# A two-layer encoder step on one core: the norms' element work at three sub-layer transitions put on VectorE alone, and the first group's read-out moved into a later m-tile

## The chip, the core and the metric

The kernel runs on one NeuronCore of a Trainium2 chip. The metric is the device time of one execution in microseconds (us), lower is better. An engine is called as the profile calls it: PE (TensorE, the matmul array), PEld (its weight loads), DVE (VectorE), ACT (ScalarE), POOL (GpSimd), SP (SyncE, which issues most DMAs).

## What is computed

The reference is one inference step of a trunk of two layers over 256 frames of a new stream and 16 frames each of 8 running streams, 384 tokens in all with 1024 features. Each layer has a mixer (even: stick-breaking attention and a gated short convolution; odd: a spatial gate and latent attention) and a squared-ReLU MLP. Around every sub-layer stand two RMS norms:

```python
h = rms_norm(x, p["mix_pre_g"][layer])
out = mixer(h)                                        # even or odd
x = x + rms_norm(out, p["mix_post_g"][layer])
h = rms_norm(x, p["ffn_pre_g"][layer])
x = x + rms_norm(sq_relu_mlp(h, w_up, w_down), p["ffn_post_g"][layer])
```

So between two sub-layers the output `out` is normed and added to `x`, `x` is normed again, and the next product starts. With two layers there are three such places inside the kernel: mixer 0 to MLP 0, MLP 0 to mixer 1, mixer 1 to MLP 1. They are called transitions here.

## The kernel before, in words

Activations lie with features on partitions: `x` is eight k-tiles of 128 features x 384 tokens. Every float32 product is made of three matmuls over two halves of each operand: a high half `h` (a rounded copy) and a low half `l` (the difference): `h*h`, `l*h`, `h*l`. Weights arrive in chunks of 512 KB by a DMA on SP; ACT casts a chunk into its high half (`whi`, line 98) and DVE subtracts to get its low half (`wlo`, line 99). Each of `raw`, `whi` and `wlo` is a ring of four buffers.

`dense` (line 296) makes one m-tile of the output after another, 8 k-tiles x 3 = 24 matmuls each over 384 columns, and reads each out with a function `evac` that its caller gives. `group` (line 271) makes the first four m-tiles of a projection side by side, so that its products of k-tile k need only that k-tile of `x`: per k-tile 8 matmuls with the high half of `x` and 4 with the low half, 96 in all. At its end all four are read out. PSUM has three tiles of tag `mm`, three of `at` and two of `aux`; the four m-tiles of a group and the next two of `dense` take all six of the first two tags.

A transition runs as follows. The last m-tile of the projection before it is squared (`OutNorm.put`, line 182), a product with ones sums the squares over the features (line 159), and ACT makes `rpost`, the reciprocal root, by Ln and Exp (lines 144, 145); meanwhile twelve matmuls that nobody reads keep PE at work (`keep_warm`, line 119). Then `Norms.prep` (line 232) does, per k-tile k: `t`, o scaled by `rpost` (line 215); `x`, added to x (line 218); `h`, the high half of gain times x, on ACT (line 221); `l`, the low half, on DVE (line 225); `s`, the square of x on ACT and its sum into `acc` on POOL (lines 168 to 172). For k = 0 the halves are made by a short way of four DVE operations (lines 242 to 245). `ORDER` (line 199) writes out in which order these steps follow on every engine; `keep` holds them to it. The other instructions (weight casts and splits) are placed between them by the framework's scheduler, which orders instructions by priority and by simulated readiness, gives out buffers, and makes the waits.

Before, `t` of k = 0 and 1, `x` of k = 0, 1, 3 and 5 and all additions of squares run on POOL, the other `t`, `x` and all `l` on DVE. When `acc` is complete, `pre_rstd` (line 264) splits it into halves (`acch` on ACT, `accl` on DVE), sums them over the features with two matmuls on PE and makes `rb` by Ln and Exp. Every read-out of the next projection multiplies by `rb`; the first one to be read out calls `pre_rstd`. In the MLP the read-out is `up` (line 402): DVE makes `h_r` (line 404), ACT its square `hh`, POOL its square again, DVE the low half `hl`. In the odd layer it is `lat` (line 699), for six m-tiles only: three of queries' latent (`qc`), two of keys' (`kv`), one of rotated keys, with the squares' sums of `qc` and `kv` for two more norms (`rkb`, `rqb`), behind which come the query products (`w_uq`); the spatial gate's product (`w_sv`) is cut into four chunks that are placed among them. `group` is used six times: at the kernel's start (`w_q`), in the three transitions (`w_up_r` twice, `w_lat_r`) and in the two output projections, whose read-out `OutNorm.put` needs no PE.

Of the kernel before, what the change touches and what calls it, by code (L numbers as in the profile page):

```python
# [15 lines left out]
P = 128  # L16
# [20 lines left out]
def encoder_step_kernel(ctx: ExitStack, tc: tile.TileContext, a):  # L37
# [26 lines left out]

# [1 line left out]
    xall = res.tile([P, KT, TOK], F32, name="x")  # L66
# [28 lines left out]

# [1 line left out]
    def split_into(hi, lo, src, eng=vec):  # L97
# [21 lines left out]
    def keep_warm(after, n):  # L119
        """PE work whose result nobody reads: an idle array drops to half its clock."""  # L120
        scratch = psum("aux")
        warm = identr.rearrange("p (r c) -> p r c", r=1).broadcast_to([P, NT, P])
        with tc.issue_after(after):
            for _ in range(n):
                mm(scratch[:, :TOK].rearrange("p (r c) -> p r c", r=NT), identr, warm, start=True, stop=True)
# [15 lines left out]

# [1 line left out]
    def rsqrt(out, src, n):  # L143
# [50 lines left out]
    class Norms:  # L194
        """x += the post-norm of o, which carries its gain; then the next sub-layer's pre-norm of x, its rstd left for
        later. Two k-tiles at a time: prep() before the products that need them, post() after."""

        # how the k-tiles follow one another on every engine: o scaled, x updated, x split in two, x squared
        ORDER = ("t1 x1 t0 x0 h1 t2 t3 x2 x3 l1 h2 s0 s1 l2 h3 t4 t5 x4 l3 s2 h4 s3 l4 x5 s4 h5 t6 x6 t7 x7 l5 s5 h6 h7 l6 "
                 "l7 s6 s7")  # L200

# [25 lines left out]
        def square(self, k):  # L227
            if k == 0:
                self.acc = wk.tile([P, TOK], F32, name="acc")
            self.last_add = square_acc(self.acc, x[k], k == 0, keep)  # L230

        def prep(self, c):
            if not self.o:
                for k in (2 * c, 2 * c + 1):
                    if k == 0:
                        vec.tensor_scalar(out=xs(k)[0], in0=x[k], scalar1=gain(self.g_pre, k), scalar2=None, op0=ALU.mult)
                    else:
                        self.hi(k)
                    self.lo(k)
            elif c == 0:  # L240
                h, l = xs(0)
                tt(out=self.b0, in0=self.b0, in1=self.r, op=ALU.mult)
                keep(tt(out=h, in0=self.a0, in1=self.b0, op=ALU.add))  # L243
                keep(tt(out=self.a0, in0=h.bitcast(F32), in1=self.a0, op=ALU.subtract))
                keep(tt(out=l, in0=self.b0, in1=self.a0, op=ALU.subtract))
                for step in self.ORDER.split():
                    k = int(step[1])
                    if step[0] == "t":
                        keep(self.scale_o(k, pool if k < 2 else vec))
                    elif step[0] == "x":  # L250
                        keep(self.add_o(k, pool if k in (0, 1, 3, 5) else vec))
                    elif step[0] == "h":
                        keep(self.hi(k))
                    elif step[0] == "l":
                        keep(self.lo(k))
                    else:
                        self.square(k)

# [10 lines left out]

# [1 line left out]
    def group(src, order, evac, norm=None, between=None, tags=("mm", "mm", "mm", "at")):  # L271
        """Four m-tiles side by side, the weights in chunks of two k-tiles."""
        pss = [psum(t) for t in tags]
        for i, c in enumerate(order):
# [14 lines left out]
            if norm:  # L289
                norm.post(c)  # L290
        for m, p_ in enumerate(pss):
            evac(m, p_[:, :TOK], ins.ins)
        wide["n"] = 4
        return ins.ins

    def dense(src, mts, rhs, nk, evac, eng=vec, tag=None):
        for i, m in enumerate(mts):
            p_ = psum(tag) if tag else psum_dense()
            for c in range(0, nk, KT):
                w = chunk(src[i] if nk <= KT else src[i, c // KT], eng=eng)  # L300
                for kk in range(min(KT, nk)):
                    k = c + kk
                    ins = mm3(p_[:, :TOK], cut(w, slice(kk * P, (kk + 1) * P)), rhs(k), k == 0, k == nk - 1)
            evac(m, p_[:, :TOK], ins.ins)

    def token_major(src, evac):
        """Tokens on partitions; stops after each of the four chunks' products."""
        pss = [psum("mm") for _ in range(NT)]
# [25 lines left out]

# [1 line left out]
    NF = 4 * KT  # L336
    LAST = 3

    def turn(k):
        """A tile of x from features to tokens on partitions, in its place."""  # L340
        pt = psum("aux")
# [4 lines left out]
    def down_last(hp, hh, hl):  # L346
        """The last product, its norm and the sum with x, tokens on partitions: one tile of tokens ends after another."""
        gb = hp.tile([P, D], F32, name="gb")
# [84 lines left out]

# [1 line left out]
    def softplus(hp, z, n, out, order=None, **dims):  # L435
# [8 lines left out]
    def even_layer(norm):  # L444
        rbs = []
        with tc.tile_pool(name="even", bufs=1) as hp:
# [21 lines left out]
            group(a["w_q"], range(4), qk, norm, between)  # L468
            rb, r = rbs
            wide["on"] = True  # L470
            dense(a["w_k"], range(4, 8), xs, KT, qk)
            wide["on"] = False
            load("ident", ident)
# [19 lines left out]
            def add_sums(z, sp, n, stop):  # L493
                """z -= the sums of sp over the keys that a row's key comes before, as two exact halves."""
                h, l = (hp.tile([P, 512], F32R, name=i, bufs=2)[:, :n] for i in ("sph", "spl"))
# [13 lines left out]
            for h in range(H):  # L509
# [3 lines left out]
                                 in_=q[p][rows, TP:].rearrange("p (b i) -> p b i", b=NB))  # L513
            # the sample's new keys against its queries, heads of one parity side by side
            po = psum("aux")
# [15 lines left out]
            nc.scalar.copy(att[:, :, TP:], po.rearrange("p (g t) -> p g t", g=NPAIR))  # L531
            # their sums, as exponents' bias for the past keys: [(h i), b]
            # (a key's row is zero but for its own stream)
            sps = hp.tile([P, P], F32, name="sps", tag="pm", bufs=2)
# [70 lines left out]
            for i in range(NB):  # L605
# [6 lines left out]
                if i % 2:  # L612
                    prompt_values(i // 2, ws[-2:])
            # gated short convolution, per tile of 128 channels
            NE = TP + 2 + NB * (TS + 2)
# [58 lines left out]

# [1 line left out]
    def rope(hp, src, dst, rows):  # L676
# [8 lines left out]
    def odd_layer(norm):  # L685
        rbs = []
        with tc.tile_pool(name="odd", bufs=1) as hp:
# [30 lines left out]
            keep(vec.tensor_copy(maskr, mask))  # L718
            rb, r = rbs
            wide["on"] = True  # L720
            dense(a["w_lat"], range(4, 6), xs, KT, lat)
            wide["on"] = False
            rkb = rstd_bcast([acck], 256, "rkb")
# [15 lines left out]

            # the spatial gate's values, tokens on partitions  # L740
            ln = hp.tile([P, 1024], F32, name="ln")
# [18 lines left out]

            # the prompt's queries and keys by head, 64 and 32 (rotated) together: rows 0-95 for even heads, 32-127 for odd
            q8 = [o[h][:, :TP] for h in range(H)]
# [7 lines left out]
            for p in range(NPAIR):  # L770
                with tc.issue_after(norm.last_add):
                    pool.memset(q8[2 * p][96:128, :], 0.0)
                    pool.memset(q8[2 * p + 1][0:32, :], 0.0)
            # the sample's: two heads' 64 in a tile's last columns; the rotated 32 as [high, low, high], [r, b, h, i]
            qn = [o[2 * p][:, TP:] for p in range(NPAIR)]
# [30 lines left out]

            # prompt keys out of the latent
            def prompt_keys():
# [11 lines left out]

            # the new latent rows, tokens on partitions
            p_ = psum("aux")
# [5 lines left out]
            vt = [hp.tile([P, 512], F32, name=f"vt{t}") for t in range(2)]  # L828
            # prompt values out of the latent
            def prompt_latent_values():  # L830
# [10 lines left out]

            # absorbed queries of the sample tokens: [c, ct, b, h, i]
            ql = []
# [69 lines left out]

            # sample attention over the past and the new rows
            def rope_keys(b):
                """Two streams' rotated keys, as [high, high, low]."""
                raw, hi = raw_tile()[0:96, :], hi_tile()[0:96, :]
# [99 lines left out]

            # the spatial gate's steps lie between the samples
            ln_at, su_at = (1, 2, 4), (2, 3, 4, 5)
# [35 lines left out]

            # spatial gating
            new_xs()
# [24 lines left out]
def _arrays(i):  # L1082
# [55 lines left out]

    # constants of the shapes
    c["ident"] = np.eye(P, dtype=f)  # L1140
# [57 lines left out]
```

## Time and profile before

| | us |
|---|---|
| median of three runs | 959.29 |
| lowest and highest run | 959.02, 960.0 |
| span of the profiled execution | 959.2 |
| PE busy in it | 927.6 (97%) |
| DVE busy | 559.6 (58%) |
| ACT busy | 392.5 (41%) |
| POOL busy | 210.7 (22%) |

The profile is of one execution; its span, from the first to the last instruction, is 959.2 us and lies within the range of the timed runs, 0.1 us under their median. Times in rows are us from the start of that span. A row of the timeline gives start, duration, engine, line, operation, output and inputs, a count when rows are merged, and in brackets the engine's idle time before it with what ended it. The duration of a matmul includes its way through the array; matmuls overlap, and the time from one start to the next is what one costs.

### The profile page before, as it was taken

The page shows a single profiled execution, that of the slowest core. Times are in us where ns is not written, and L with a number is a line of the kernel's source. Part 1 is how long each engine was busy: PE and PEld are TensorE (multiplying, and loading weights), DVE is VectorE, ACT ScalarE, POOL GpSimd, SP SyncE. Part 2 cuts the span into 40 slices and gives each one's busy share as a digit, 9 for nine tenths or more (in the row PEclk, how much of TensorE's full clock was granted, in tenths as well). Part 3 has the DMA queues.
Part 4 walks back from the last instruction along what each step waited for, and adds up shares of the span by engine and source line. Part 5 has one row for each costly group of instructions (what it writes and reads, how often), then busy time and mean ns, then how long its engine had stood idle before and what let it go on. Part 6 is the DMA issues. An engine that isn't in the chain of part 4 may idle for free.

```text
span 959.2 us, 13748 instructions
## 1 busy us (share of the span) xinstructions
PE 927.6 (97%) x5328; PEld 849.5 (89%) x5328; DVE 559.6 (58%) x798; ACT 392.5 (41%) x661; POOL 210.7 (22%) x236
## 2 busy tenths in 40 slices
PE   8999999989999999999979989999799999999997
PEld 6976679978999999999969779989699999888885
DVE  7457675578666643323396788664976666332234
ACT  6256553345333332222245665553453334222222
POOL 4200113345312210001055314003642212000000
PEclk9999999999999999999999999999999999999999
DMA  7957733323333433333322646454243333334322
GB/s 244 356 178 254 254 131 127 121 85 110 132 119 124 132 133 116 126 132 125 118 96 85 190 145 220 154 177 132 68 141 121 132 131 111 122 121 132 130 68 66
DMA packets 44593, 135.64 MB, mean 141 GB/s; under 512 B 5264, under 2 KB 10768, under 8 KB 44528
## 3 DMA queue, kind: packets, MB, share of 16 engines
q1 hardware_dynamic: 42128, 131.53, 41.4%
q0 software_dynamic: 816, 2.45, 0.7%
q8 instruction: 42, 0.69, 0.3%
q10 hardware_dynamic: 1584, 0.79, 0.3%
q14 instruction: 23, 0.19, 0.1%
HBM read 130.20 MB, written 3.89 MB: 140 GB/s over the span
## 4 chain that ended last, share of the span: by engine, by line
PE 87%; DVE 9%; issue 1%; ACT 1%; DMA 1%; SPq 0%; POOL 0%; DVEq 0%
PE ps_mm L135 10%; PE ps_mm L136 10%; PE ps_mm L137 10%; PE ps_at L135 8%; PE ps_at L136 8%; PE ps_at L137 8%; PE ps_mm L359 2%; PE ps_at L359 2%; PE ps_at L358 2%; PE ps_mm L357 2%; PE ps_mm L358 2%; PE ps_at L357 2%; PE ps_aux L982 2%; DVE o L215 2%; DVE xl L225 2%; PE ps_mm L288 1%
## 5 line engine op out<-in xcount | busy, mean ns | idle before, releaser
L99 DVE TENSOR_TENSOR wlo<-raw,whi 128x1024 fp32r<-128x1024 f32 (+3 forms) x200 | 264.9, 1327 | 246.5 <-ACT whi L98 245.2
L98 ACT CAST whi<-raw 128x1024 fp32r<-128x1024 f32 (+3 forms) x200 | 204.9, 1026 | 399.9 <-issue 137.6
L135 PE MATMUL ps_mm<-xh,whi 128*128 128x384 f32 x396 | 134.5, 340 | 0.0
L137 PE MATMUL ps_mm<-xh,wlo 128*128 128x384 f32 x396 | 133.9, 338 | 0.0
L136 PE MATMUL ps_mm<-xl,whi 128*128 128x384 f32 x396 | 133.7, 338 | 0.0
L172 POOL TENSOR_TENSOR acc<-acc,sq 128x384 f32<-128x384 f32 x48 | 66.8, 1392 | 203.5 <-ACT sq L171 200.7
L409 POOL TENSOR_TENSOR h<-h_r 128x384 f32<-128x384 f32 x64 | 58.5, 916 | 185.1 <-DVE h_r L404 185.1
L135 PE MATMUL ps_at<-xh,whi 128*128 128x384 f32 x284 | 95.9, 338 | 0.0
L136 PE MATMUL ps_at<-xl,whi 128*128 128x384 f32 x284 | 95.7, 337 | 0.0
L137 PE MATMUL ps_at<-xh,wlo 128*128 128x384 f32 x284 | 95.6, 337 | 0.0
L135 PEld LDWEIGHTS ps_mm<-xh,whi 128*128 128x128 f32 x396 | 74.4, 188 | 3.0 <-issue 1.9
L136 PEld LDWEIGHTS ps_mm<-xl,whi 128*128 128x128 f32 x396 | 74.4, 188 | 2.1 <-issue 1.8
L137 PEld LDWEIGHTS ps_mm<-xh,wlo 128*128 128x128 f32 x396 | 74.3, 188 | 1.9 <-issue 1.7
L136 PEld LDWEIGHTS ps_at<-xl,whi 128*128 128x128 f32 x284 | 53.3, 188 | 0.0
L135 PEld LDWEIGHTS ps_at<-xh,whi 128*128 128x128 f32 x284 | 53.3, 188 | 0.0
L137 PEld LDWEIGHTS ps_at<-xh,wlo 128*128 128x128 f32 x284 | 53.3, 188 | 0.0
L285 PE MATMUL ps_mm<-xh,whi 128*128 128x384 f32 x132 | 45.7, 349 | 5.1 <-DVE xh L243 3.0
L286 PE MATMUL ps_mm<-xh,wlo 128*128 128x384 f32 x132 | 45.1, 344 | 1.8 <-DVE wlo L99 1.8
L288 PE MATMUL ps_mm<-xl,whi 128*128 128x384 f32 x132 | 32.5, 351 | 11.4 <-DVE xl L225 8.7
L135 PE MATMUL ps_mm<-hh,whi 128*128 128x384 f32 x128 | 43.2, 337 | 0.0
L136 PE MATMUL ps_mm<-hl,whi 128*128 128x384 f32 x128 | 43.2, 337 | 0.0
L137 PE MATMUL ps_mm<-hh,wlo 128*128 128x384 f32 x128 | 43.2, 337 | 0.0
(370 smaller groups left out, 1856.9 us busy)
## 6 DMA issues: line engine op xcount, KB each, us to landing
raw<-in_w_up SPq DMA_DIRECT2D x56, 512.0 KB, 3.5
raw<-in_w_down SPq DMA_DIRECT2D x32, 512.0 KB, 3.5
raw<-in_w_down_last SPq DMA_DIRECT2D x32, 512.0 KB, 3.5
kc<-in_sb_kT SPq DMA_DIRECT2D x16, 512.0 KB, 5.6
vc<-in_sb_v SPq DMA_DIRECT2D x16, 512.0 KB, 5.4
raw<-in_w_conv_in SPq DMA_DIRECT2D x12, 512.0 KB, 5.4
raw<-in_w_up_r SPq DMA_DIRECT2D x8, 512.0 KB, 3.5
raw<-in_ckvT SPq DMA_DIRECT2D x8, 512.0 KB, 4.3
```

The costliest lines, as they stand in the source:

```text
L98: nc.scalar.copy(hi, src)
L99: eng.tensor_tensor(out=lo, in0=src, in1=hi.bitcast(F32), op=ALU.subtract)
L135: mm(out, w[0], x_[0], start=start, stop=False)
L136: mm(out, w[0], x_[1], start=False, stop=False)
L137: return mm(out, w[1], x_[0], start=False, stop=stop)
L172: added = pool.tensor_tensor(out=acc, in0=acc, in1=sq, op=ALU.add)
L285: mm(p_[:, :TOK], w_[0], h, start=first, stop=False)
L286: mm(p_[:, :TOK], w_[1], h, start=False, stop=False)
L288: ins = mm(p_[:, :TOK], w_[0], l, start=False, stop=last)
L357: mm(out, hh[k][:, sl], hi, start=(k == 0), stop=False)
L358: mm(out, hh[k][:, sl], lo, start=False, stop=False)
L409: pool.tensor_tensor(out=h2, in0=h_r, in1=h_r, op=ALU.mult)
```

## The change

All three transitions: `t` and `x` run on DVE for every k. `ORDER` goes k by k from 1 to 7, with `l` one step behind `h`; squares (`s`, ACT alone) follow, and the additions of squares are steps of their own (`a`, DVE), put at the end together with k = 0's `t`, `x` and `s`. `acc` starts as the square of k = 1. `group` no longer reads out its m-tiles but leaves that in a list, `later`; the first m-tile of the `dense` that follows puts its own read-out there too; and in the second m-tile, after the matmuls of its k-tile 4 (`nk // 2`), the list is worked off, PE's instructions in it being ordered behind those matmuls. `rb, r = rbs` moves behind the `dense` call in both mixers. `norm.last_add`, behind which ten POOL memsets of the odd layer are ordered, is now a DVE instruction.

```diff
-        ORDER = ("t1 x1 t0 x0 h1 t2 t3 x2 x3 l1 h2 s0 s1 l2 h3 t4 t5 x4 l3 s2 h4 s3 l4 x5 s4 h5 t6 x6 t7 x7 l5 s5 h6 h7 l6 "
-                 "l7 s6 s7")
+        ORDER = ("t1 x1 h1 t2 x2 h2 l1 t3 x3 h3 l2 s1 t4 x4 h4 l3 s2 t5 x5 h5 l4 s3 t6 x6 h6 l5 s4 t7 x7 h7 l6 l7 a2 s5 a3 s6 "
+                 "a4 s7 t0 x0 a5 s0 a6 a7 a0")
...
         def square(self, k):
             if k == 0:
                 self.acc = wk.tile([P, TOK], F32, name="acc")
-            self.last_add = square_acc(self.acc, x[k], k == 0, keep)
+            square_acc(self.acc, x[k], k == 0, keep)
+
+        def square_alone(self, k):
+
+            if k == 1:
+                self.acc = self.sq[k] = wk.tile([P, TOK], F32, name="acc")
+            else:
+                self.sq[k] = wk.tile([P, TOK], F32, name="sq", tag="t15", bufs=4)
+            keep(act(out=self.sq[k], in_=x[k], func=AF.Square))
+
+        def add_square(self, k):
+            self.last_add = keep(tt(out=self.acc, in0=self.acc, in1=self.sq[k], op=ALU.add)).ins
...
                     if step[0] == "t":
-                        keep(self.scale_o(k, pool if k < 2 else vec))
+                        keep(self.scale_o(k, vec))
                     elif step[0] == "x":
-                        keep(self.add_o(k, pool if k in (0, 1, 3, 5) else vec))
+                        keep(self.add_o(k, vec))
...
+                    elif step[0] == "s":
+                        self.square_alone(k)
                     else:
-                        self.square(k)
+                        self.add_square(k)
...
+    later = []
+
     def group(src, order, evac, norm=None, between=None, tags=("mm", "mm", "mm", "at")):
...
-        for m, p_ in enumerate(pss):
-            evac(m, p_[:, :TOK], ins.ins)
+        def leave():
+            for m, p_ in enumerate(pss):
+                evac(m, p_[:, :TOK], ins.ins)
+
         wide["n"] = 4
-        return ins.ins
+        later.append(leave)
 
     def dense(src, mts, rhs, nk, evac, eng=vec, tag=None):
...
                     ins = mm3(p_[:, :TOK], cut(w, slice(kk * P, (kk + 1) * P)), rhs(k), k == 0, k == nk - 1)
-            evac(m, p_[:, :TOK], ins.ins)
+                    if i == 1 and k == nk // 2:
+                        with tc.issue_after(ins.ins):
+                            while later:
+                                later.pop(0)()
+            if i == 0 and later:
+                later.append(lambda m=m, p_=p_, ins=ins: evac(m, p_[:, :TOK], ins.ins))
+            else:
+                evac(m, p_[:, :TOK], ins.ins)
...
             group(a["w_q"], range(4), qk, norm, between)
-            rb, r = rbs
             wide["on"] = True
             dense(a["w_k"], range(4, 8), xs, KT, qk)
+            rb, r = rbs
...
             group(a["w_lat_r"], range(4), lat, norm)
             keep(vec.tensor_copy(maskr, mask))
-            rb, r = rbs
             wide["on"] = True
             dense(a["w_lat"], range(4, 6), xs, KT, lat)
+            rb, r = rbs
```

The rest of the diff removes comments and docstrings.

## Rows read from the trace of the kernel before

**Rows 1.** The page, its first part: busy time of each engine, share, instructions.

```profile
PE 927.6 (97%) x5328; PEld 849.5 (89%) x5328; DVE 559.6 (58%) x798; ACT 392.5 (41%) x661; POOL 210.7 (22%) x236
```

**Rows 2.** Windows, three transitions: length, PE, PEld, DVE, ACT, POOL busy, PEclk, DMA.

```profile
203.57:228.06 24.49, 19.12 (x102) 17.26 (x101) 21.79 (x25) 10.25 (x19) 17.14 (x13) 1.00 0.20 63
483.37:509.40 26.03, 20.69 (x103) 18.80 (x102) 22.94 (x26) 10.80 (x19) 19.44 (x17) 0.93 0.18 59
672.66:697.15 24.49, 19.14 (x102) 17.27 (x101) 21.78 (x25) 10.25 (x19) 17.15 (x13) 1.00 0.28 87
```

**Rows 3.** Timeline of ACT, steady state of MLP 0.

```profile
241.19 1.05 ACT L98 CAST whi<-raw 128x1024 fp32r<-128x1024 f32 x1 [0.27 <-PE ps_mm L136]
...
245.41 1.05 ACT L98 CAST whi<-raw 128x1024 fp32r<-128x1024 f32 x1 [1.62 <-PE ps_mm L136]
```

**Rows 4.** Timeline of PE, first transition: its five waits, then pre_rstd.

```profile
205.46 0.44 PE L285 MATMUL ps_mm<-xh,whi 128*128 128x384 f32 x1 [1.01 <-DVE xh L243]
208.03 0.79 PE L288 MATMUL ps_mm<-xl,whi 128*128 128x384 f32 x3 [0.90 <-DVE xl L245]
211.53 0.80 PE L288 MATMUL ps_mm<-xl,whi 128*128 128x384 f32 x3 [1.12 <-DVE xl L225]
219.57 0.45 PE L285 MATMUL ps_mm<-xh,whi 128*128 128x384 f32 x1 [0.54 <-ACT xh L221]
223.03 0.79 PE L288 MATMUL ps_mm<-xl,whi 128*128 128x384 f32 x3 [1.79 <-DVE xl L225]
228.06 0.34 PE L159 MATMUL ps_aux<-acch,ponesr 128*128 128x384 f32 x1
```

**Rows 5.** Timeline of DVE, first transition.

```profile
203.57 0.56 DVE L242 TENSOR_TENSOR b<-b,rpost 128x384 f32<-128x384 f32 x1
204.17 1.24 DVE L243 TENSOR_TENSOR xh<-a,b 128x384 fp32r<-128x384 f32 x1
...
214.51 0.55 DVE L218 TENSOR_TENSOR x<-x,o 128x384 f32<-128x384 f32 x1
214.98 0.60 DVE L225 SCALAR_TENSOR_TENSOR xl<-x,small,xh 128x384 fp32r<-128x384 f32 x1
215.51 1.21 DVE L99 TENSOR_TENSOR wlo<-raw,whi 128x1024 fp32r<-128x1024 f32 x1
```

**Rows 6.** Lines by form, 203 to 229: busy us, mean ns | idle before, releaser.

```profile
L172 POOL TENSOR_TENSOR acc<-acc,sq 128x384 f32<-128x384 f32 x7 | 9.6, 1368 | 5.2 <-ACT sq L171 5.0
...
L215 DVE TENSOR_TENSOR o<-o,rpost 128x384 f32<-128x384 f32 x6 | 7.2, 1229 | 0.0
...
L225 DVE SCALAR_TENSOR_TENSOR xl<-x,small,xh 128x384 fp32r<-128x384 f32 x7 | 5.5, 822 | 0.0
...
L221 ACT ACTIVATE xh<-x,small 128x384 fp32r<-128x384 f32 x7 | 4.3, 612 | 11.0 <-DVE x L218 5.9 <-POOL x L218 5.1
...
L218 DVE TENSOR_TENSOR x<-x,o 128x384 f32<-128x384 f32 x4 | 2.9, 724 | 0.1
...
L99 DVE TENSOR_TENSOR accl<-acc,acch 128x384 fp32r<-128x384 f32 x1 | 0.6, 561 | 2.5 <-ACT acch L98 2.5
...
L98 ACT CAST acch<-acc 128x384 fp32r<-128x384 f32 x1 | 0.5, 513 | 3.2 <-POOL acc L172 3.2
```

**Rows 7.** Windows, inside the second transition (columns as in rows 2).

```profile
503.00:506.40 3.40, 3.40 (x12) 3.40 (x13) 1.97 (x3) 0.73 (x2) 2.87 (x2) 0.50 0.10 23
```

**Rows 8.** Timeline of four engines, behind the second transition's group.

```profile
510.01 0.58 ACT L144 ACTIVATE rb<-ps_aux,epst 128x384 f32<-128x384 f32 x1
...
510.67 0.52 ACT L145 ACTIVATE rb<-rb 128x384 f32<-128x384 f32 x1
...
518.83 0.81 PE L159 MATMUL ps_aux<-acck,ones 128*128 128x384 f32 x2
...
524.83 0.52 PE L135 MATMUL ps_at<-qch,whi 128*128 128x384 f32 x2
...
510.14 0.56 DVE L99 TENSOR_TENSOR wlo<-raw,whi 128x384 fp32r<-128x384 f32 x1 [0.47 <-ACT whi L98]
...
510.31 0.31 POOL L772 MEMSET o<- 32x256 f32 x1
```

More of the change, by code (lines that the diff above doesn't have):

```diff
@@ L245, in prep @@
                 keep(tt(out=l, in0=self.b0, in1=self.a0, op=ALU.subtract))
+                self.sq = {}
                 for step in self.ORDER.split():
```

## The prediction
> **What bounds the kernel now.** The page's first part comes first: PE is busy 97% of the span [rows 1], so time can only come from places where PE stands still or runs slowly, or be lost there. The chain of waits and the table of waits then point to three such places, the transitions: from the sum that gives `rpost` to the last product of the next group of four m-tiles. The windows view [rows 2] shows their length: 24.49, 26.03 and 24.49 us, with VectorE busy 21.8 to 22.9 us and GpSimd 17 to 19 us of each. A group is 8 k-tiles x 12 products = 96 matmuls. At PE's steady pace, 4.22 us from one weight cast to the next, each after an m-tile of 24 products [rows 3], one product takes 0.176 us, so the group needs 16.9 us of the 24.49. PE's own timeline [rows 4] shows the rest: five waits of 1.01, 0.90, 1.12, 0.54 and 1.79 us, four on VectorE and one on an `xh` whose `x` came from GpSimd, plus filling up after each.
>
> Why VectorE is late is read from durations. The same 128x384 operation takes 0.55 to 0.60 us with GpSimd idle (L218 at 214.51, L225 at 214.98) and 1.24 us beside it (L243 at 204.17) [rows 5]; the group means, 1229, 822 and 724 ns, are mixtures of the two [rows 6]. So GpSimd's help is paid for twice: its own adds take 1.37 us [rows 6], and VectorE's operations beside them double.
>
> In the second transition the clock fell too: the granted clock is 0.50 from 503.0 to 506.4, the lower level, 1.2 GHz [rows 7], after a stretch with those five waits. That transition is 1.54 us longer than its twins [rows 2].
>
> **The change, part by part.** Set t = 0 where L242 starts (203.57 in the first transition, 483.37 in the second) [rows 5]. On VectorE an operation that needs the one before it starts 0.60 later (L242 to L243), an independent one 0.47 later (L218 to L225) and one behind an L225 0.53 later (L225 to L99) [rows 5].
>
> *GpSimd leaves.* Its 2 scalings, 4 residuals and 7 square sums move to VectorE: 13 operations at about 0.55. In return the 25 operations of the chain up to the last `xl` (4 of the head, 7 each of t, x, l) lose their neighbour. I take 0.55 to 0.60 for all of them; bounds are 0.55 (never a neighbour) and 1.24 to 1.36 (always), and the nearest rows are those with GpSimd idle, since nothing of the transition stays there.
>
> *PE's new course.* xh0 is ready at 0.60 + 0.56, and PE starts at 1.20 (before: 1.89) [rows 4]. xl0 comes at 2.4, in time for k=0's last four products. Then t1 at 2.27, x1 at 2.87 to 3.43, h1 on ScalarE 0.61 [rows 6] to 4.08: PE waits about 0.8 us and starts k=1 at 4.13. From here VectorE needs t + x + l = 0.60 + 0.47 + 0.53 = 1.60 us per k-tile against PE's 12 x 0.176 = 2.11: PE leads the pace. The group ends at 4.13 + 7 x 2.11 = 18.9 instead of 24.49: **5.6 us saved**. The cover: two to three weight splits of 1.2 us [rows 5] in VectorE's queue still leave the last `xl` at about 17, needed at 18.2. Were that slack gone, each missing microsecond would be PE's.
>
> *The square sums now end late.* After l7 VectorE still has 7 adds, t0 and x0: 9 x 0.6 = 5.4, and another split or two: 22.4 to 23.5; with the cast and the low half of `acc` (0.51 + 0.56) [rows 6] and handovers 23.6 to 24.7. Read out at the group's end as now, that would hold PE from 18.9 on. The deferral puts the two products of pre_rstd behind k=4 of the second m-tile: 18.9 + 4.2 + 2.6 = 25.7. Slack 1 to 2 us, so the sums cost nothing while it lasts.
>
> *The wait that comes in.* Four PSUM tiles of the group and two of m-tiles fill all six; the third m-tile needs the first read out. `rb` comes at 25.7 + 0.35 + Ln and Exp 1.2 [rows 8] = 27.3, the read-out lasts to 27.9; PE is through the second m-tile at 18.9 + 8.4 + 0.35 = 27.6. PE waits 0.25. Later read-outs need to keep one tile per 4.2 us, which the steady state does already. Behind these waiting read-outs on VectorE stand only the weight splits of later chunks. **Net per MLP transition 5.6 - 0.25 = 5.35, twice: 10.7 us**; bounds 3 (slack gone) and 5.6.
>
> *The second transition* (odd layer) gains 5.6 + 1.54 = 7.1 at the group's end, if with fewer waits the clock stays up. But behind it lies a chain of short steps that the deferral feeds later: only two m-tiles follow. pre_rstd starts at 483.37 + 25.7 = 509.1 and `rb` ends some 0.3 us before the 511.19 of now [rows 8]; then come five read-outs, their squares and GpSimd's adds, and the sum for `rkb` can start at about 515.6 (now 518.83, behind PE's own queue) [rows 8]; the query products start 6.0 us later (524.83 now) [rows 8]: 521.7. PE has the first chunk of `w_sv` as filling from 511.6 to 516 and then nothing for up to 5 us. So at most 3.2 us get through in this reading. Such an idle stretch may bring the lower clock for a while as in [rows 7], whose price was 1.54. I take 2.3, between 1.5 and 3.2; outer bounds 0 and 7.1.
>
> The Trainium skill, "TensorE: Matmul & The Clock Gate", section "What's actually happening", says that the throttled clock is the default and that activity releases it. The fall in this trace after a stretch of waits agrees; by that rule the lower clock moves from the transition to the queries, and the odd layer keeps about 1.5: the sum would be 947.1 instead of 946.3.
>
> *Edits at nothing.* Ten memsets of the odd layer were ordered behind GpSimd's last add; that add is VectorE's now, so nothing orders them and they may run during the transition. A 384-column split with two inputs took 0.56 beside one [rows 8], so they don't slow VectorE. The first group (`w_q`) and the two output projections also have their read-outs deferred. PE has two m-tiles of 8.4 us to run meanwhile; the projections' read-outs hold no PE work, so they are free to go at once, and their sum is asked for four m-tiles later. For `w_q`, the first key tile's output DMA on GpSimd's queue moves with the read-out, with the whole projection of `w_v` left before attention. I take 0, bounds -0.3 (better) and +1.0 (its `rb` shares ScalarE with a weight cast of 1.05 [rows 3]). SyncE's queue gets nothing new.
>
> **Sum**: 959.2 - 10.7 - 2.3 = 946.2 on the profiled span; the median of the runs is 0.1 above that: **946.3 us**.
>
> **Rivals.**
> *A, the odd layer keeps everything.* If the scheduler finds PE other work for 516 to 521, or the chain to the queries contracts, 7.1 instead of 2.3: 941.5. Against: the weight ring has four slots and the query weights come before the next `w_sv` chunk. 13%.
> *B, slack gone.* The splits land in the wrong places of VectorE's fixed order, `acc` comes 2 us late, PE waits mid-tile: about 2 us left per transition: 953. 8%.
> *C, slower: VectorE stays slow.* If 1.24 is not GpSimd's doing but these operations' own, the chain to l7 is 25 x 1.33 + 3 x 1.2 = 37 us, the group ends at 38 instead of 24.5: 13 us lost three times, 999. It decides from a mean of 0.85 us per operation, where the chain is as long as now. Against it stand L218 and L225 with GpSimd idle [rows 5]. 7%, with lesser losses in it.
> The Trainium skill, "Perfetto Trace Analysis", section "Optimizing Scalar/DVE Operations", says that with VectorE saturated some work may be offloaded, even to GpSimd, though the two share a read port so that it might not help. By the first half alone this change loads a saturated engine further, as in C, 999; the trace (1.24 beside, 0.55 alone) bears out the second half, as in the forecast.
> *D, no change.* The read-out's place is only an order among PE instructions; if the sums arrive so late that PE waits out all it gained, 959. 5%.
>
> **How the numbers follow.** The forecast has 67%; with A and B it makes 88% faster. A measurement of this kernel can tell about 0.2%, 1.9 us, from no change. The range takes in A and the forecast with an odd layer at 0 and MLP transitions at 4: 959.3 - 8 = 951.3. That leaves B's worse half, C and D out.
>
> **What would show it.** Right: VectorE's L215, L218, L225 and the three head operations near 0.55 to 0.60; no GpSimd work in the MLP transitions; PE with one wait near h1 and then none to the group's end, 18.9 us after L242; pre_rstd in the middle of the second m-tile with no wait before it; a wait under 0.5 us on the first `h_r`. In the odd layer: idle PE before the first query product, perhaps with a clock of 0.5 behind it. Wrong: waits of PE on `accl`, or on `xh`/`xl` past k=1, or durations above 0.9.

## The result and the profile after

The changed kernel takes 949.07 us (median of 4 runs, 947.76 to 951.11) against 959.64 for the kernel before beside it (4 runs, 959.02 to 963.54): a ratio of 0.9882, interval 0.9857 to 0.9906. Timed again beside the experiments it took 948.91 (6 runs) against 961.58 (11 runs): 0.9865, interval 0.9843 to 0.9887. So it is faster, by 11 to 13 us, and the time lies in the forecast's range. The profiled execution has a span of 946.2 us.

The page's first part, against [rows 1]: PE is as busy as before, GpSimd has lost 49 us, and VectorE has as much to do as it had, although 39 operations moved to it.

```profile
PE 924.8 (98%) x5328; PEld 849.4 (90%) x5328; DVE 555.0 (59%) x837; ACT 392.4 (41%) x661; POOL 161.6 (17%) x197
```

Why moved work costs VectorE nothing shows in its timeline (first transition) and in the lines by form of 203 to 229, against [rows 5, 6].

```profile
203.40 0.56 DVE L253 TENSOR_TENSOR b<-b,rpost 128x384 f32<-128x384 f32 x1
204.00 0.56 DVE L254 TENSOR_TENSOR xh<-a,b 128x384 fp32r<-128x384 f32 x1
...
226.86 0.56 DVE L99 TENSOR_TENSOR accl<-acc,acch 128x384 fp32r<-128x384 f32 x1 [0.58 <-ACT acch L98]
```

```profile
L218 DVE TENSOR_TENSOR x<-x,o 128x384 f32<-128x384 f32 x8 | 4.5, 556 | 0.2
L215 DVE TENSOR_TENSOR o<-o,rpost 128x384 f32<-128x384 f32 x8 | 4.4, 552 | 0.0
...
L225 DVE SCALAR_TENSOR_TENSOR xl<-x,small,xh 128x384 fp32r<-128x384 f32 x7 | 4.3, 612 | 0.2 <-ACT xh L221 0.2
L241 DVE TENSOR_TENSOR acc<-acc,sq 128x384 f32<-128x384 f32 x7 | 3.9, 555 | 0.2
```

The second operation of the head takes 0.56 us instead of 1.24; `t` 552 ns instead of 1229, `x` 556 instead of 724, `l` 612 instead of 822. `accl` is done at 227.42, 24.0 us after the start of the head, the four operations of k = 0 (L242 to L245 before, L253 to L256 now); 23.6 to 24.7 was forecast.

PE's timeline of the same transition, all its waits from the head to the third m-tile, and the deferred `pre_rstd` between:

```profile
204.61 0.45 PE L301 MATMUL ps_mm<-xh,whi 128*128 128x384 f32 x1 [0.34 <-DVE xh L254]
...
207.51 0.44 PE L301 MATMUL ps_mm<-xh,whi 128*128 128x384 f32 x1 [0.54 <-ACT xh L221]
...
229.12 0.34 PE L159 MATMUL ps_aux<-acch,ponesr 128*128 128x384 f32 x1
...
231.46 0.45 PE L135 MATMUL ps_mm<-xh,whi 128*128 128x384 f32 x1 [0.25 <-DVE h_r L429]
```

Of the five waits of [rows 4] only the first is left, with 0.34 us instead of 1.01; one of 0.54 before the products of `h1` is new, as the prediction said. As windows, the first group, and then head to `pre_rstd` in the first and the second transition (columns as in rows 2):

```profile
203.40:222.30 18.90, 18.02 (x102) 17.38 (x101) 18.42 (x33) 9.96 (x17) 0.00 (x0) 1.00 0.25 84
203.40:229.12 25.72, 24.84 (x141) 24.20 (x140) 23.95 (x41) 12.89 (x21) 0.00 (x0) 1.00 0.31 103
477.96:504.80 26.84, 25.13 (x141) 24.17 (x140) 22.96 (x42) 11.95 (x21) 2.33 (x8) 1.00 0.23 74
```

The group takes 18.90 us where it took 24.49 [rows 2], with nothing on GpSimd. The second transition is 1.1 us longer than the first, which the odd layer below explains.

To see where the time went, the span is cut where each transition's first operation (L242 before, L253 now) starts. The table has the experiments in it too, by what each runs; the stretch from the first transition to the second holds MLP 0, the next the odd layer, the last MLP 1.

| | start to 1st | 1st to 2nd | 2nd to 3rd | 3rd to end | span |
|---|---|---|---|---|---|
| before | 203.57 | 279.80 | 189.29 | 286.54 | 959.2 |
| after | 203.40 | 274.56 | 187.22 | 281.02 | 946.2 |
| after, another execution | 203.84 | 274.55 | 189.16 | 280.95 | 948.5 |
| read out at the group's end | 203.66 | 274.34 | 184.05 | 281.05 | 943.1 |
| the same, another execution | 203.85 | 274.35 | 183.92 | 281.08 | 943.2 |
| deferral alone | 203.36 | 280.10 | 194.51 | 286.53 | 964.5 |
| read out after two m-tiles | 206.98 | 278.20 | 188.94 | 282.18 | 956.3 |
| order of before, read out at the end | 204.19 | 275.44 | 184.14 | 282.13 | 945.9 |
| with reads on GpSimd | 203.87 | 278.10 | 190.96 | 284.57 | 957.5 |
| with writes on GpSimd | 203.43 | 275.03 | 188.97 | 281.47 | 948.9 |
| mask's cast later | 203.49 | 274.55 | 187.06 | 281.00 | 946.1 |

After against before: 5.24 us in MLP 0, 2.07 in the odd layer, 5.52 in MLP 1, 0.17 at the start. Together 13.0. The 0.17 is no gain: two executions of the changed kernel differ by 0.44 in that column. All profiles but that of the deferral alone have one stretch of the lower clock between 556 and 574 us, in the latent attention (0.53 in the window 560 to 562 of the changed kernel's); the stretches that the text speaks of come on top of it.

### The profile page after: what moved, and what is told of

Read it like the earlier page. It is cut to its first block, busy times and chain, and to the rows that moved or that the text cites. A ratio compares the mean times of both kernels' runs of the same rounds, so it can differ in the third digit from the quotient of the medians.

```text
span 946.2 us, 13719 instructions
## 1 busy us (share of the span) xinstructions
PE 924.8 (98%) x5328; PEld 849.4 (90%) x5328; DVE 555.0 (59%) x837; ACT 392.4 (41%) x661; POOL 161.6 (17%) x197
## 4 chain that ended last, share of the span: by engine, by line
PE 91%; DVE 5%; ACT 1%; DMA 1%; issue 1%; POOL 0%; SPq 0%; DVEq 0%
PE ps_mm L135 10%; PE ps_mm L137 10%; PE ps_mm L136 10%; PE ps_at L136 8%; PE ps_at L135 8%; PE ps_at L137 8%; PE ps_mm L384 2%; PE ps_at L384 2%; PE ps_mm L382 2%; PE ps_at L383 2%; PE ps_mm L383 2%; PE ps_at L382 2%; PE ps_mm L301 2%; PE ps_mm L302 2%; PE ps_mm L304 2%; PE ps_aux L1007 2%
## 5 line engine op out<-in xcount | busy, mean ns | idle before, releaser
L137 PE MATMUL ps_mm<-xh,wlo 128*128 128x384 f32 x396 | 133.9, 338 | 0.0
L136 PE MATMUL ps_mm<-xl,whi 128*128 128x384 f32 x396 | 133.6, 337 | 0.0
L434 POOL TENSOR_TENSOR h<-h_r 128x384 f32<-128x384 f32 x64 | 61.6, 966 | 227.6 <-DVE h_r L429 195.6
L137 PE MATMUL ps_at<-xh,wlo 128*128 128x384 f32 x284 | 95.6, 337 | 0.0
L137 PEld LDWEIGHTS ps_mm<-xh,wlo 128*128 128x128 f32 x396 | 74.3, 188 | 1.9 <-issue 1.7
L172 POOL TENSOR_TENSOR acc<-acc,sq 128x384 f32<-128x384 f32 x27 | 38.5, 1424 | 214.5 <-ACT sq L171 213.7
L137 PEld LDWEIGHTS ps_at<-xh,wlo 128*128 128x128 f32 x284 | 53.3, 188 | 0.0
L137 PE MATMUL ps_mm<-hh,wlo 128*128 128x384 f32 x128 | 43.2, 337 | 0.0
L135 PE MATMUL ps_at<-hh,whi 128*128 128x384 f32 x128 | 43.2, 337 | 0.0
```

Source lines behind the costliest of these rows:

```text
L135: mm(out, w[0], x_[0], start=start, stop=False)
L136: mm(out, w[0], x_[1], start=False, stop=False)
L137: return mm(out, w[1], x_[0], start=False, stop=stop)
L172: added = pool.tensor_tensor(out=acc, in0=acc, in1=sq, op=ALU.add)
L434: pool.tensor_tensor(out=h2, in0=h_r, in1=h_r, op=ALU.mult)
```

## Experiments on VectorE's speed: work put back on GpSimd

If the gain is VectorE running without a neighbour, then work on GpSimd that reads SBUF must take it away again, even work that nobody needs, and work that only writes must not. Both kernels issue it behind the head, into a tile that nobody reads then.

```diff
+                for _ in range(8):
+                    keep(pool.tensor_tensor(out=self.b0, in0=self.r, in1=self.r, op=ALU.mult))
```

> The changed kernel with eight more operations on GpSimd in each transition, two-input products over rpost (128x384, about 1.3 us each), written to a tile that nobody reads; nothing else waits for them. Theory (GpSimd's reading beside VectorE doubles VectorE's two-input operations): L215, L218 and L225 that run beside them take 1.2 to 1.4 us instead of 0.55 to 0.61, some nine of them are hit, 6 us on VectorE of which the slack takes 1 to 2: the group ends 23 to 24 us after L253's line starts instead of 18.9, span 956 to 961. Rival (VectorE was slow for another reason, such as its own dependences or the order): durations stay at 0.55 to 0.61, span within 1 us of 946.2.

Measured: 959.19 us, one run; against the changed kernel +3.5, +3.7 and +3.6 us in the three stretches. The timeline of GpSimd and of VectorE beside it:

```profile
206.35 8.71 POOL L258 TENSOR_TENSOR b<-rpost 128x384 f32<-128x384 f32 x8 [6.42 <-DVE xl L256]
```

```profile
206.12 0.55 DVE L215 TENSOR_TENSOR o<-o,rpost 128x384 f32<-128x384 f32 x1
206.71 1.06 DVE L218 TENSOR_TENSOR x<-x,o 128x384 f32<-128x384 f32 x1
...
214.29 1.18 DVE L215 TENSOR_TENSOR o<-o,rpost 128x384 f32<-128x384 f32 x1
215.50 0.56 DVE L218 TENSOR_TENSOR x<-x,o 128x384 f32<-128x384 f32 x1
```

Every VectorE operation from 206.71 to 215.5 takes 1.06 to 1.18 us, and the first one behind GpSimd's eighth is back at 0.56. The group's last product starts 22.3 us after the head where the changed kernel's starts at 18.75; its end was expected at 23 to 24. Eight operations that compute nothing needed thus give back 3.5 us of the 5.2 to 5.5. The rest they can't show: the kernel before had thirteen operations on GpSimd there, and another order.

The writes: one such reading operation, then thirty memsets.

```diff
+                keep(pool.tensor_tensor(out=self.b0, in0=self.r, in1=self.r, op=ALU.mult))
+                for _ in range(30):
+                    keep(pool.memset(self.b0, 0.0))
```

> As the run with eight reading operations, but one of them followed by thirty memsets of the same tile: GpSimd is busy and writes, but reads nothing. Theory (it is the reading that collides): VectorE's operations stay at 0.55 to 0.61 beside the memsets but for one or two beside the first operation, span 946 to 948. Rival (any work of GpSimd slows VectorE): 1.2 to 1.4 us as with reads, span 956 or more.

Measured: 950.61 us, somewhat over what was expected. GpSimd's timeline and VectorE's:

```profile
205.91 1.01 POOL L257 TENSOR_TENSOR b<-rpost 128x384 f32<-128x384 f32 x1 [6.42 <-DVE xl L256]
206.98 14.26 POOL L259 MEMSET b<- 128x384 f32 x30
```

```profile
206.27 1.06 DVE L218 TENSOR_TENSOR x<-x,o 128x384 f32<-128x384 f32 x1
207.26 0.55 DVE L215 TENSOR_TENSOR o<-o,rpost 128x384 f32<-128x384 f32 x1
207.84 0.56 DVE L218 TENSOR_TENSOR x<-x,o 128x384 f32<-128x384 f32 x1
208.31 0.61 DVE L225 SCALAR_TENSOR_TENSOR xl<-x,small,xh 128x384 fp32r<-128x384 f32 x1
```

The only slow operation, 1.06, is beside the one that reads; beside 14.26 us of memsets all run at full speed. That one delay falls on `x1`, just ahead of `h1` for which PE waits, and costs about 0.45 us in each MLP stretch; the odd layer has a stretch of the lower clock in this execution (0.50 in the window 518 to 520), which the changed kernel's profile has not at that place. So reading is what counts, and a busy GpSimd as such is not. The Trainium skill says the same ("SBUF — State Buffer", section "Who interferes with whom"): a VectorE instruction with two inputs in SBUF contends with a GpSimd instruction that reads SBUF, and not with one that only writes; both runs agree, with 1.06 to 1.18 us beside the reads and 0.55 to 0.61 beside the writes.

## An experiment on the order

All of the work on VectorE as in the change, but in before's `ORDER`, each addition right behind its square, and the read-out at the group's end.

```diff
-        ORDER = ("t1 x1 h1 t2 x2 h2 l1 t3 x3 h3 l2 s1 t4 x4 h4 l3 s2 t5 x5 h5 l4 s3 t6 x6 h6 l5 s4 t7 x7 h7 l6 l7 a2 s5 a3 s6 "
-                 "a4 s7 t0 x0 a5 s0 a6 a7 a0")
+        ORDER = ("t1 x1 t0 x0 h1 t2 t3 x2 x3 l1 h2 s0 s1 l2 h3 t4 t5 x4 l3 s2 h4 s3 l4 x5 s4 h5 t6 x6 t7 x7 l5 s5 h6 h7 l6 "
+                 "l7 s6 s7")
...
-            if k == 1:
+            if k == 0:
...
+                        if k:
+                            self.add_square(k)
...
-        later.append(leave)
+        leave()
```

> Everything on VectorE as in the changed kernel and read out at the group's end, but in the order of the kernel before (each addition of a square right behind its square). It tells the move from GpSimd apart from the new order. Theory (the move alone frees VectorE's operations, but in the old order t0, x0, the pairs of t and x and the additions stand ahead of l1 and l5, so PE waits about 1.4 and 2.2 us for these two): group's end about 22.5 us after the first of the head operations, against 24.5 before and 18.9 in the changed kernel, hence some 2 us gained per MLP transition instead of 5.3; span 950 to 954. Rival A (the order is worth nothing once GpSimd is out): 943 to 945. Rival B (the move is worth nothing without the order): 957 or more.

Measured: 947.26 us (4 runs, 945.0 to 947.78), ratio 0.9846, interval 0.9822 to 0.987; span 945.9. The old order costs less than was expected: beside the same read-out with the new order, 1.1 us in each MLP stretch and 0.1 in the odd layer. (The 0.3 to 0.5 us more at the start are not the order's: no step of it runs there, and PE waits 1.00 us at 10.80 for an `xh` whose `x` comes by DMA.) PE's timeline says why it is so little:

```profile
211.11 0.79 PE L306 MATMUL ps_mm<-xl,whi 128*128 128x384 f32 x3 [1.13 <-DVE xl L225]
...
219.78 0.33 PE L304 MATMUL ps_at<-xh,wlo 128*128 128x384 f32 x1
219.96 0.33 PE L137 MATMUL ps_at<-xh,wlo 128*128 128x384 f32 x1
...
222.04 0.68 PE L306 MATMUL ps_mm<-xl,whi 128*128 128x384 f32 x3
```

One wait, 1.13 us, is left uncovered. At 219.96 a product of the next m-tile (L137, of `dense`) stands between two halves of the group's own k-tile: the scheduler put 14 such products into the group (2 at 218.22, 12 up to 222.04), where PE would have waited for an `xl` that this order makes late. The group's last product does come late, 22.6 us after the head, about where it was expected; but by then those 14 products are done. So most of the gain is the move to VectorE, and the new order is worth about 2.2 us of it, the two MLP stretches. The medians differ by about as much (947.26 and 944.82), though single runs of the two overlap.

## Experiments on the deferral

The changed kernel, with the group's read-out at its end as before:

```diff
-        later.append(leave)
+        leave()
```

> The changed kernel, but the group's four m-tiles are read out in program order at the group's end, as before; the new order on VectorE stays. In the changed kernel's trace the low half of acc is ready 24.0 us after VectorE starts L253, the group ends on PE at 18.9. Theory A (the deferral is not what saves the time: left alone, the scheduler sets the two products of pre_rstd behind the first following m-tile, at about 18.9 + 4.2 = 23.1, so PE waits under 1 us there and the 0.25 us wait on the first read-out goes): span within 1 us of the changed kernel's 946.2 or up to 2 us shorter, since in the odd layer rb comes some 1.5 us sooner and the chain to the query products with it. Rival B (as I had it in the prediction: read out at the end, PE is held from 18.9 to 24.0): 5 us lost in each of three transitions, span about 960.

Measured: 945.73 us (4 runs, 944.4 to 946.73) against 961.84: 0.9834, interval 0.9807 to 0.9861. It was timed again beside the changed kernel, on the same chip:

> The changed kernel itself, on the same chip as the run without its deferral. Theory (the deferral costs time in the odd layer and next to nothing elsewhere): span 945 to 948, about 3 us longer than the run without the deferral; from L253 of the second transition to that of the third 187.2 us against 184.0. Rival (the 3 us between the two profiles are scatter of single executions): medians within 1 us of each other.

> The changed kernel read out at the group's end, once more, beside the changed kernel on one chip. Theory: 3 us shorter than it, all of it between the second and the third transition; a faster kernel than both. Rival: within 1 us of it.

Measured: the changed kernel 948.91 us (947.43 to 950.59), the read-out at the end 944.82 (4 runs, 944.67 to 946.22; ratio to before 0.9829, interval 0.9805 to 0.9852). The intervals of the two ratios overlap by a little, the runs themselves do not. In the table the MLP stretches are alike to within 0.25 us, and the whole difference, 3.2 us, lies in the odd layer. So the deferral buys nothing and costs 3 to 4 us. PE's timeline in the first transition, then in the odd layer, and a row of VectorE's there:

```profile
227.13 0.44 PE L159 MATMUL ps_aux<-acch,ponesr 128*128 128x384 f32 x1
...
227.94 0.34 PE L159 MATMUL ps_aux<-accl,ponesr 128*128 128x384 f32 x1
...
509.02 0.91 PE L159 MATMUL ps_aux<-acck,ones 128*128 128x384 f32 x2 [0.87 <-POOL acck L172]
...
513.67 0.69 PE L135 MATMUL ps_at<-qch,whi 128*128 128x384 f32 x3
```

```profile
505.68 1.03 DVE L743 CAST maskr<-pr 128x384 fp32r<-128x384 f32 x1
```

No wait is listed at `pre_rstd`. The scheduler had put its two products behind 25 and 28 products of the next two m-tiles by itself, about where `acc` is ready (24.0 us after the head), 1.6 to 2.2 us ahead of the deferral's place (25.7). In the odd layer this brings the sum for `rkb` to 31.0 us after the head, where the changed kernel has it at 34.2, and the first query product to 35.7 instead of 38.8. One more thing differs there: the cast of the attention's mask, of which the section on the odd layer speaks, stands 27.7 us after the head here (505.68), and in the changed kernel 2.0 us after it, inside the head.

The deferral without the rest, on the kernel before:

```diff
-        for m, p_ in enumerate(pss):
-            evac(m, p_[:, :TOK], ins.ins)
+        def leave():
+            for m, p_ in enumerate(pss):
+                evac(m, p_[:, :TOK], ins.ins)
+
...
+        later.append(leave)
...
```

The cut part has the edits to `dense` and to the two mixers as in the change.

> The kernel before with the deferral alone; its order and its work on GpSimd stay. Theory: the group is held by VectorE as before (24.5 us), so nothing is gained in the MLP transitions, 0.25 us is lost in each on the first read-out, and in the odd layer rb comes some 7 us later after the group's end, the sum for rkb some 4 us later: span 962 to 965. Rival (the deferral is worth something by itself because read-out and VectorE's late work no longer meet): below 958.

Measured: 966.25 us, one run, span 964.5, as expected. In the MLP stretches it changes 0.30 and 0.01 us; the odd layer takes 5.2 us longer. The loss is again in that layer alone.

Last the read-out still later, at the end of the second m-tile:

```diff
-                    if i == 1 and k == nk // 2:
+                    if i == 1 and k == nk - 1:
```

> The changed kernel with the read-out deferred to the end of the second m-tile (behind k-tile 7 instead of 4), 9 products or 1.6 us later. Theory (all six PSUM tiles are taken, so the third m-tile waits for the first read-out): PE's wait on the first h_r grows from 0.25 to about 1.9 us in the MLPs (less in the second, where transposes fill some of it), and the odd layer's chain starts 1.6 us later: span 949 to 952. Rival (a tile is free, or other work fills the gap): within 1 us of 946.2.

Measured: 958.07 us, one run, far over what was expected. PE's timeline at the kernel's first group and in the first transition, and a window behind the latter:

```profile
36.41 0.48 PE L135 MATMUL ps_mm<-xh,whi 128*128 128x384 f32 x1 [1.78 <-DVE o L482]
36.69 0.52 PE L136 MATMUL ps_mm<-xl,whi 128*128 128x384 f32 x1
...
237.13 0.44 PE L135 MATMUL ps_mm<-xh,whi 128*128 128x384 f32 x1 [2.34 <-DVE h_r L429]
```

```profile
238.20:241.60 3.40, 3.40 (x13) 3.40 (x12) 3.15 (x5) 1.05 (x2) 2.37 (x3) 0.52 0.33 119
```

The wait for the read-out is 2.34 us instead of 0.25, and in the first group, where the changed kernel has no such wait, 1.78. Behind each of the two the granted clock is at the lower level for some 3.4 us (one product per 0.32 us from 36.69 on, instead of one per 0.176), which costs about 1.6 more: 1.78 + 1.6 is the 3.6 us of the first stretch, 2.34 - 0.25 + 1.6 the 3.6 of the second. With a third such stretch in the odd layer the clock makes up about half of the 10.1 us by which the span grew. So the deferral's place at k = 4 has no slack: the first `h_r` is waited for there already, and 1.6 us later (`pre_rstd` at 27.3 us after the head instead of 25.7) the wait and its clock cost 3.6 us in MLP 0; MLP 1, which has no such stretch of the clock, loses 1.2.

## Experiments on the odd layer

The changed kernel's second transition has waits that the first has not. VectorE's timeline, then PE's:

```profile
478.55 0.56 DVE L254 TENSOR_TENSOR xh<-a,b 128x384 fp32r<-128x384 f32 x1
479.91 0.45 DVE L743 CAST maskr<-pr 128x384 fp32r<-128x384 f32 x1 [0.80 <-DMA pr<-in_mla_mask]
480.28 0.54 DVE L255 TENSOR_TENSOR a<-xh,a 128x384 f32<-128x384 f32 x1
```

```profile
481.46 0.79 PE L304 MATMUL ps_mm<-xl,whi 128*128 128x384 f32 x3 [0.64 <-DVE xl L256]
...
512.18 0.91 PE L159 MATMUL ps_aux<-acck,ones 128*128 128x384 f32 x2 [1.42 <-POOL acck L172]
...
516.71 0.80 PE L135 MATMUL ps_at<-qch,whi 128*128 128x384 f32 x3 [0.87 <-ACT qch L98]
```

The cast of the attention's mask (`vec.tensor_copy(maskr, mask)`, whose order is kept) was placed inside the head, and stands there for a DMA, with the rest of the head behind it: the group takes 20.04 us instead of 18.9. It is the deferral that brings it there: the program has the cast behind `group`, which no longer holds the read-outs. Wherever the deferral stands without the edit below it starts 1.5 to 2.2 us after the head's start, in the kernel before and in those read out at the group's end 26 to 30 us after it. In the execution with the span of 948.5 it waits longer, and then the lower clock follows within the transition (window of PE's products right behind):

```profile
480.59 0.36 DVE L743 CAST maskr<-pr 128x384 fp32r<-128x384 f32 x1 [1.04 <-DMA pr<-in_mla_mask]
```

```profile
484.10:487.50 3.40, 3.40 (x12) 3.40 (x11) 3.33 (x8) 1.64 (x3) 0.00 (x0) 0.51 0.00 0
```

That execution has 189.16 us for the odd layer, 1.94 more than the other, and as much as the kernel before, whose transition had such a stretch as well [rows 7]. One experiment moves the cast behind the last addition:

```diff
-            keep(vec.tensor_copy(maskr, mask))
...
+            with tc.issue_after(norm.last_add):
+                vec.tensor_copy(maskr, mask)
```

> The changed kernel with one edit: the cast of the odd layer's attention mask is ordered behind the last addition of squares instead of keeping its place right behind the group. Theory: in the changed kernel this cast stands between the second and the third operation of the odd transition's head and waits 0.80 us for its DMA, which lengthens the group's course on PE from 18.9 to 20.04 us; without it the stretch from the second transition's first operation to the third's shrinks by about 1.1 us, from 187.22 to 186.1, and the span from 946.2 to about 945.1. The rest of the 3 us by which reading out at the group's end beats the changed kernel in that layer (187.22 against 184.05) is the late pre_rstd and stays. Rival: the whole 3 us is the cast, which also starts the lower clock in some executions: the stretch falls to about 184.2 and the span to 943.2. Second rival: the 1.1 us is given back at the queries, which wait for the key path anyway: the stretch stays at 187.2 though the group takes 18.9.

Measured: 948.39 us (4 runs, 946.9 to 949.22), ratio 0.9861, interval 0.9836 to 0.9886; span 946.1, odd layer 187.06. The group's waits are gone and the first query product comes 37.6 us after the head instead of 38.8. But the second rival holds: the layer is no shorter. The lead lasts through the latent attention's first batches and ends here (timelines of PE, ACT and SP's queue, attention over the past):

```profile
602.44 0.30 PE L993 MATMUL ps_aux<-ident,pn 128*128 128x128 f32 x1 [0.71 <-DVE ol L1010]
```

```profile
598.87 1.07 ACT L98 CAST whi<-raw 128x1056 fp32r<-128x1056 f32 x1 [1.84 <-DMA raw<-in_ckvT]
```

```profile
594.81 0.55 SPq L959 DMA_DIRECT2D raw<-in_ckvT  x1
```

At this place the changed kernel has no wait. VectorE reaches that copy in both at about 124 us after the head, behind a weight split that waits for ACT, so PE's lead turns into a wait there. ACT in turn waits for a DMA that SP issues 116.8 us after the head here, 116.6 in the changed kernel, and 113.3 in the kernel read out at the group's end. So that kernel's 3 us are not lost at this place because its DMA goes out 3 us sooner too. What holds the issue back when the cast alone moves was not traced further. Of the 3.1 us by which that kernel's first query product comes sooner, 1.1 go with the cast's place, which alone shortens nothing (187.06 against 187.22), and the other 1.9 with the sooner `pre_rstd`.

## Why the prediction was right, and where it was not

**Right, with its sizes.** VectorE's durations (0.55 to 0.61), PE's start, k = 1 at 4.11 us (forecast 4.13), the group of 18.90 (18.9), `accl`, `pre_rstd` at 25.72 (25.7), the wait for the first `h_r` of 0.25 (0.25), and the MLP transitions, 5.24 and 5.5 (5.35). The cause, VectorE slowed by a GpSimd that reads, was argued from rows; the two experiments on GpSimd show it. The sum of 13.0 is what the two profiled spans differ by; the medians of the timed runs differ by 10.6 and 12.7.

**Wrong: the place of the read-out.** "Read out at the group's end as now, that would hold PE from 18.9 on" does not hold: the scheduler orders the two products behind the first that can run, and the read-out at the end is 3 to 4 us faster. I took the program's order for PE's order, in a kernel whose order comes from a scheduler. The front part says so; the step did not use it.

**Right by luck: the odd layer.** 2.3 was forecast and 2.07 measured, but the parts differ. The sum for `rkb` was put at 32.2 us after the head, without a sum of its parts, and comes at 34.2; from there to the query products 6.0 were taken from before and 4.5 are measured, so that those come at 38.8 (forecast 38.3). PE waits 2.8 us on that way in four pieces, not 5, and no lower clock follows. The sum also assumed a clean transition. Instead the deferral let a kept instruction that waits for a DMA slip into the head (1.1 us), which is not among the edits at nothing, and 1.5 of the 2.07 is the stretch of lower clock that before's profile had [rows 7] and after's, by chance, had not. With such a stretch in both (189.29 and 189.16) the odd layer gains 0.1 us; without the deferral it gains 5.2, or some 3.7 where before's 1.54 is set aside. So it was the deferral, by the later `pre_rstd` and by the cast, that kept the chain to the queries from contracting, which was rival A's condition. Nor do the five waits bring the lower clock by themselves, as the prediction reads [rows 7]: the first and third transitions of the kernel before have the same waits at a clock of 1.00 [rows 2].

**Wrong by 1.6 us: from span to time.** Every execution that has both has its time 1.7 to 1.9 us above its span (947.91 and 946.2). The prediction, like the front part, put the span of before beside the median of other runs and read 0.1. By the same 1.7 the profiled execution of before stands for about 960.9. The forecast of 946.3 lies 2.8 under the median of 949.07: 1.6 from this step, and 1.2 because the profiled execution is one of the shorter ones.

**Nothing, as forecast:** the first group (0.17 us, within its scatter) and the odd layer's memsets, which now run from 475.3 to 480.0, just before the second transition's head and beside it; there L253 and L254 take 0.56.

## What to carry to other kernels

An operation handed to GpSimd is paid for on VectorE as well where both read SBUF (0.55 us alone, 1.06 to 1.24 beside it here): compare the same operation's duration with GpSimd idle and busy before calling VectorE full. Where a scheduler orders the instructions, look in the trace where it put a waiting product before moving that by hand; a fixed later place takes the early finish from the chain behind it. And before a gain of 2 us is read from two profiles, count the stretches of lower clock in each.

## What was not expected of the hardware

Which of the two engines is slowed depends on which starts first. A weight split of 1024 columns, also of two inputs, shows it in MLP 0 of the kernel before, where GpSimd squares `h_r` beside it (VectorE's and GpSimd's timelines):

```profile
243.15 1.22 DVE L99 TENSOR_TENSOR wlo<-raw,whi 128x1024 fp32r<-128x1024 f32 x1
...
254.93 1.66 DVE L99 TENSOR_TENSOR wlo<-raw,whi 128x1024 fp32r<-128x1024 f32 x1 [0.39 <-ACT whi L98]
```

```profile
243.38 1.67 POOL L409 TENSOR_TENSOR h<-h_r 128x384 f32<-128x384 f32 x1 [1.21 <-DVE h_r L404]
...
254.68 0.83 POOL L409 TENSOR_TENSOR h<-h_r 128x384 f32<-128x384 f32 x1 [3.40 <-DVE h_r L404]
```

Where GpSimd's row begins 0.23 us behind the split's, the split takes 1.22 us and GpSimd 1.67; where it begins 0.25 ahead, GpSimd takes 0.83 and the split 1.66. In the kernel before 50 splits have one operation of GpSimd that begins 0.20 to 0.26 ahead, and they take 1.65 to 1.70; the 21 beside which the first one begins only after their start take 1.21 to 1.23. The Trainium skill ("SBUF — State Buffer", section "Who interferes with whom") says that the order of issue decides which of the two blocks the other; these rows agree. Rows of GpSimd are rough, and four places do not fit; in the first transition, an addition at 223.66 begins 0.30 ahead of a split that still takes 1.22. In the first group, whose additions of squares stay on GpSimd, a split beside them takes 2.04 us, and PE waits 1.21 for it (0.80 in the changed kernel); the change leaves that place as it is.

The second thing is that a wait of PE can cost twice: in the kernel that reads out after two m-tiles, 1.78 and 2.34 us of standing still each have some 3.4 us at the lower clock behind them, worth about 1.6 us more.
